# RWKV-7 chunk products on whole 128x128 stationaries, with the group norm's tokens on partitions

## The chip, the cores and the metric

One core of a Trainium2 chip runs the whole program in one launch. The metric is device time in microseconds (us). Five engines take part: TensorE (PE, matmuls, with its weight loads listed as PEld), VectorE (DVE), ScalarE (ACT), GpSimd (POOL) and SyncE (SP), on whose queue all DMAs are issued.

## The reference

One step of a one-layer decoder trunk for 256 prompt tokens and 8 sample sequences of 8 tokens, 320 token columns in all. Three branches (HGRN2, RWKV-7, a short gated convolution) are computed from one input projection, merged by gates, projected, and followed by an MLP. The change is in the RWKV-7 branch, with 16 heads of 64 channels:

```python
def step(S, inp):                      # per token; S is (B, H, 64, 64), [value, key]
    r_, w_, k_, v_, kk_, a_ = inp
    sa = einsum('bhij,bhj->bhi', S, -kk_)
    S = S * w_[:, :, None, :] + sa[..., None] * (kk_ * a_)[:, :, None, :] + v_[..., None] * k_[:, :, None, :]
    return S, einsum('bhij,bhj->bhi', S, r_)
...
mu = mean(o_rw, -1); var = mean(square(o_rw - mu), -1)         # per token and head
o_rw = ((o_rw - mu) * rsqrt(var + 64e-5)) * rw_ln_w + rw_ln_b
bonus = sum(r_ * k_ * rw_r_k, -1) * v_
y_b = ((o_rw + bonus) * g) @ w_pb
```

## The kernel before

Activations lie feature-major: 128 channels on partitions, 320 token columns (256 of the prompt, 64 of the samples). Weights come by DMA in granules of 8 blocks of 128x128 (`granule`, lines 107 to 116). ScalarE casts each granule to a high part `whi_t` (line 104), VectorE subtracts to get the low part `wlo_t` (line 105), and `dense` (lines 118 to 132) issues three matmuls for each block into `mm_t` (lines 128 to 130). These dense matmuls make up most of TensorE's work. Three buffers hold each of raw, high and low parts.

The RWKV branch runs first, with the projections of the short convolution among it. It handles two heads (128 channels) at a time, eight pairs `j`. For each pair:

- `rwkv_front` projects keys, receptances and values, and forms for five chunks of 64 tokens (four of the prompt, one that holds all samples) the operands: `LYR` (alpha, from the decay and kk, and rho, from the receptance), `BK` and its transposed form `BT`, and `X`, which holds token-major values beside the state or the intermediate u. `vx` becomes the bonus term.
- `rwkv_solve` forms the products inside each chunk (line 441, operands of 64 partitions), masks them into `Nb`, `LYR` and `GB`, and inverts I - N into `Pm`.
- `rwkv_chunks` goes through the four prompt chunks in order. For each chunk: alpha times `X` into `yp` (line 534), rho times `X` as the first half of the output in `op` (line 536), a copy `Y` on ScalarE (line 538), `Pm` times `Y` (line 543), two copies on VectorE that put u into `X` (line 545), the new state (line 548), the second half of the output (line 550), and the state with its decay into `X` of the next chunk (lines 555 and 557). Then come the sample chunk (lines 561 to 585) and the group norm (lines 593 to 610).

In the chunk products each head has its own matmul with a stationary operand of 64 columns. The two heads write the two halves of the partitions of one PSUM bank. The output is feature-major, so the norm's mean and variance are products with the block matrix `bo64` (lines 597 and 602), and all its arithmetic runs over 320 columns, a reciprocal among it (`rsqrt`, line 162).

The source fixes which engine does each operation. The order of the queues is not written out: when the program is built, a planner orders each engine's instructions by their dependencies and its own estimate of costs, and it interleaves the dense matmuls of one pair with the small products of another. `X`, `LYR`, `BT` and `W` have two buffers, so front and solve of later pairs run beside the chunks of an earlier one. The tiles `py_t` and `po_t` have one PSUM bank each.

Of the kernel before, what the change touches and what calls it, by code (L numbers as in the profile page):

```python
# [16 lines left out]
# Columns of every feature-major tile: 256 prompt tokens, then 8 sample  # L17
# sequences of 8 tokens each.
# [8 lines left out]
# Tile indices (128 columns each) inside w_in.  # L27
# [5 lines left out]
# Columns of the packed per-channel parameters.  # L33
# [10 lines left out]
# words between two diagonal 16x16 blocks of a [128, 640] array  # L44
# [5 lines left out]
def _constants():  # L50
    """Identity, block matrices and masks: they depend on shapes alone."""
# [6 lines left out]
    cols["bo64"] = cols["bo1"] / 64.0  # L58
    up, upi = (s % 64 < q), (s % 64 <= q)
    same = (s % 64) // 8 == q // 8  # L60
    cols["mkp"] = np.concatenate([up, upi, up], 1)
    cols["mks"] = np.concatenate([up & same, upi & same, up & same], 1)
# [24 lines left out]
class K:  # L87
# [19 lines left out]
    def granule(self, src, pool=None):  # L107
        """8 weight blocks of 128x128 as float32r high and low parts."""
        raw = self.wraw.tile([128, 1024], F32, name="raw")
        self.nc.sync.dma_start(raw, src)  # L110
        hi = (pool or self.whi).tile([128, 1024], F32R, name="whi_t")
        lo = (pool or self.wlo).tile([128, 1024], F32R, name="wlo_t")
        for q in range(2):
            c = slice(512 * q, 512 * q + 512)
            self.split(hi[:, c], lo[:, c], raw[:, c])
        return hi, lo

    def dense(self, granules, ah, al):
        """PSUM tile = sum over the granules of weight block ^T @ activation block."""
# [14 lines left out]
    def dense_wide(self, tiles, ah, al, psp, wpool):  # L134
        """Several column tiles at once, one activation block after the other."""
# [19 lines left out]
    def rsqrt(self, pool, v, tag):  # L155
        """1/sqrt(v): table square root, reciprocal, one Newton step."""
# [12 lines left out]
    # -----------------------------------------------------------------------  # L169
    def build(self):  # L170
# [41 lines left out]
        # operands of the sample sequences' new states wait in DRAM  # L212
# [40 lines left out]
    def shift_mix(self, wp, n, name, packed):  # L253
        """Projected tile n with the token shift mixed in; keeps the last rows."""
# [22 lines left out]
    def rwkv(self, cx):  # L277
# [16 lines left out]
        # tiles whose constant blocks are written once  # L294
# [4 lines left out]
        for nm, cols in (("Nb", 640), ("GB0", 640), ("GB1", 640), ("LX", 256)):  # L299
            Z[nm] = kp.tile([128, cols], F32, name=nm)  # L300
            nc.gpsimd.memset(Z[nm], 0.0)
# [3 lines left out]
        # DRAM scratch through which the diagonal 16x16 blocks change layout  # L305
# [27 lines left out]
    def rwkv_front(self, j, wp, w2):  # L333
# [9 lines left out]
        # decay, gate and rate from the low-rank projections  # L343
# [20 lines left out]
        # normalised kk, k with its rate  # L364
# [8 lines left out]
        LYR = w2.tile([128, 5, 2, 2, 64], F32, name="LYR")  # L373
# [3 lines left out]
        V.tensor_mul(LYR[lo, :, 0, 0, :], ch(Wp)[lo], ch(kkn)[lo])  # L377
        V.tensor_mul(LYR[hi, :, 1, 1, :], ch(Wp)[hi], ch(kkn)[hi])
        G.tensor_mul(LYR[lo, :, 0, 1, :], ch(W)[lo], ch(r)[lo])
        G.tensor_mul(LYR[hi, :, 1, 0, :], ch(W)[hi], ch(r)[hi])  # L380
# [10 lines left out]
        # token-major values: X holds [state or u ; v] per chunk and head  # L391
# [16 lines left out]
        V.tensor_mul(vx, bs[:, :NT], vx)  # L408

        # token-major [beta ; kappa]  # L410
# [10 lines left out]
    def rwkv_solve(self, j, front, wp):  # L421
# [7 lines left out]
        # pairwise products inside each chunk  # L429
        Nb = Z["Nb"].rearrange("p (c w) -> p c w", w=128)  # L430
        GB = Z["GB%d" % (j % 2)].rearrange("p (c h w) -> p c h w", h=2, w=64)
        for mk, cc in (("mkp", slice(0, 4)), ("mks", slice(4, 5))):
# [5 lines left out]
            for i in range(n):  # L438
                c = cc.start + i
                for h, rows in ((0, lo), (1, hi)):  # L440
                    T.matmul(pp[h][:, i, :], BK[rows, c, h:h + 2, :].rearrange("p a w -> p (a w)"),  # L441
                             LYR[rows, c, h].rearrange("p a w -> p (a w)"), start=True, stop=True)
            for h, rows in ((0, lo), (1, hi)):
                p3 = pp[h]
                orow = hi if h == 0 else lo
                ca = lo if h == 0 else hi        # columns of alpha
                cr = hi if h == 0 else lo        # columns of rho
                m = self.cst(mk)[:, 64 * h:64 * h + 128]
                mc = lambda rr, col: m[rr, col].unsqueeze(1).to_broadcast([64, n, col.stop - col.start])
                full = slice(0, 128)  # L450
                V.tensor_mul(Nb[rows, cc, ca], p3[rows, :n, ca], mc(rows, ca))
                V.tensor_mul(LYR[orow, cc, h].rearrange("p c a w -> p c (a w)"), p3[orow, :n, :], mc(orow, full))
# [4 lines left out]
        # P = (I - N)^-1: diagonal 16x16 blocks first, each on one partition  # L457
# [21 lines left out]
        # then doubling, with M = P^T  # L479
# [31 lines left out]
    def rwkv_chunks(self, j, front, wp, w2):  # L511
# [13 lines left out]
        # prompt chunks in order  # L525
        op = self.po.tile([128, 512], F32, name="po_t")
        Y = wp.tile([128, 64], F32, name="Y")
        Sw = wp.tile([128, 64], F32, name="Sw")
        heads = ((0, lo), (1, hi))
        for c in range(4):  # L530
            wc = W[:, c * 64 + 63:c * 64 + 64]
            yp = self.py.tile([128, 512], F32, name="py_t")
            for h, rows in heads:
                T.matmul(yp[rows, 0:64], LYR[:, c, h, h, :], X[:, c, h, :], start=True, stop=True)
            for h, rows in heads:
                T.matmul(op[rows, c * 64:c * 64 + 64], X[:, c, h, :], LYR[:, c, h, 1 - h, :],
                         start=True, stop=False)
            S.copy(Y, yp[:, 0:64])
# [8 lines left out]
            for h, rows in heads:  # L547
                T.matmul(sp[rows, 0:64], BT[:, c, h, :], X[:, c, h, :], start=True, stop=True)
            for h, rows in heads:
                T.matmul(op[rows, c * 64:c * 64 + 64], X[:, c, h, :], GB[:, c, h, :], start=False, stop=True)  # L550
            sn = wp.tile([128, 64], F32, name="sfin")
            for h, rows in heads:
                dst = X[rows, c + 1, h, :] if c < 3 else sn[rows, :]
                if c:
                    V.scalar_tensor_tensor(dst, sp[rows, 0:64], wc[rows], Sw[rows, :], ALU.mult, ALU.add)
                else:
                    V.tensor_scalar_mul(dst, sp[rows, 0:64], wc[rows])
# [3 lines left out]
        LX = Z["LX"].rearrange("p (b h a t) -> p b h a t", h=2, a=2, t=8)  # L561
        for h, rows in heads:
            S.copy(LX[rows, :, h], LYR[rows, 4, h].rearrange("p a (b t) -> p b a t", t=8))
        cp = self.pa.tile([128, 512], F32, name="pa_t")
        for b in range(8):
            T.matmul(cp[lo, b * 32:b * 32 + 32], s0[:, b, :], Z["LX"][:, b * 32:b * 32 + 32],
                     start=True, stop=True)
        cpv = cp[lo, 0:256].rearrange("p (b h a t) -> p b h a t", h=2, a=2, t=8)
        YA = wp.tile([64, 2, 64], F32, name="YA")
        YR = wp.tile([128, 64], F32, name="YR")  # L570
        t8 = lambda t: t.rearrange("p (b t) -> p b t", t=8)
        for h, rows in heads:
            S.copy(t8(YA[:, h, :]), cpv[:, :, h, h, :])
            S.copy(t8(YR[rows, :]), cpv[:, :, h, 1 - h, :])
        yp = self.py.tile([128, 512], F32, name="py_t")
        for h, rows in heads:
            T.matmul(yp[rows, 0:64], LYR[:, 4, h, h, :], X[:, 4, h, :], start=True, stop=False)
            T.matmul(yp[rows, 0:64], YA[:, h, :], ident[lo, lo], start=False, stop=True)
        S.copy(Y, yp[:, 0:64])
        up = self.py.tile([128, 512], F32, name="py_t")  # L580
        T.matmul(up[:, 0:64], Pm[:, 4, :], Y, start=True, stop=True)
        for h, rows in heads:
            V.tensor_copy(X[rows, 4, h, :], up[rows, 0:64])
        for h, rows in heads:
            T.matmul(op[rows, 256:320], X[:, 4, h, :], GB[:, 4, h, :], start=True, stop=True)
# [536 lines left out]
```

## Time and profile before

| | |
|---|---|
| time of 3 runs, median (lowest to highest) | 2500.53 us (2499.78 to 2504.2) |
| profiled execution, span from the first to the last instruction | 2502.3 us |
| mean granted clock of TensorE | 0.992 |
| moved by DMA | 355.02 MB, mean 142 GB/s |

The page gives no other time of the profiled execution than its span; the median of the runs lies 0.07% under it. Rows of the profile give busy time of an engine; for TensorE the listed length of a matmul overlaps with the next one's, so the distance between two starts tells what one costs. Names such as `py_t<-X,LYR 128*64 128x64` give the tile written, the tiles read, rows and columns of the stationary operand, and the shape of the moving one. A float32 product shows as two instructions (x2), a transpose as one. Rows of groups end with busy us, mean ns of one, and idle us before them with what ended the idle time.

### The profile page before, as it was taken

Reading aid. Unit: us, or ns where it says so; the run is one execution under the profiler, and the core shown is the slowest. Engines: PE = TensorE matmul, PEld = TensorE weight load, DVE = VectorE, ACT = ScalarE, POOL = GpSimd, SP = SyncE. Lnnn points to the kernel's source line nnn. Section 1 sums busy time; section 2 is a strip of 40 time slices with the busy share of each in tenths; the row PEclk is TensorE's granted clock in tenths of the full one; section 3 lists DMA queues with packets and bytes.
Section 4 is the critical chain, followed back from the end, with each engine's and each line's share of the span. In section 5 each row is a group of like instructions: output and inputs, shape, how many; then the busy total and the mean of one; then the engine's idle time right before and its main releaser. Section 6 shows DMA issues by size and latency. Waiting matters only on the chain.

```text
span 2502.3 us, 42443 instructions
## 1 busy us (share of the span) xinstructions
PE 2456.1 (98%) x16588; PEld 2337.3 (93%) x16588; DVE 1523.7 (61%) x3022; ACT 980.0 (39%) x1882; POOL 409.4 (16%) x558
## 2 busy tenths in 40 slices
PE   8999999999999999999999999899999999999998
PEld 7887888889999999999999897899999999999997
DVE  6878888786565665565555445854555555555555
ACT  5433434433433333343444334434333333333333
POOL 5423333231000000011111233400000000000003
PEclk9999999999999999999999999899999999999999
DMA  6333333334434344344444655444444444444443
GB/s 215 120 84 89 99 112 122 115 124 127 138 129 137 129 137 131 127 143 148 151 152 147 214 189 184 131 149 151 152 148 150 149 152 152 147 149 151 152 150 129
DMA packets 131703, 355.02 MB, mean 142 GB/s; under 512 B 34864, under 2 KB 43440, under 8 KB 131504
## 3 DMA queue, kind: packets, MB, share of 16 engines
q1 hardware_dynamic: 131504, 352.32, 43.1%
q8 instruction: 131, 2.15, 0.4%
q14 instruction: 68, 0.56, 0.1%
HBM read 337.13 MB, written 15.14 MB: 141 GB/s over the span
## 4 chain that ended last, share of the span: by engine, by line
PE 89%; DVE 7%; POOL 1%; DMA 1%; issue 1%; SPq 0%; ACT 0%; POOLq 0%; DVEq 0%; ACTq 0%
PE mm_t L128 27%; PE mm_t L129 26%; PE mm_t L130 26%; DVE wlo_t L105 1%; PE pi L501 1%; DMA Pm<-dP 1%; PE pi L441 1%; PE pho_t L805 1%; PE plv_t L765 1%; DVE x L941 1%; PE pi L507 1%; PE plv_t L766 0%; DVE hl L943 0%; DVE xl L200 0%; PE po_t L550 0%
## 5 line engine op out<-in xcount | busy, mean ns | idle before, releaser
L104 ACT CAST whi_t<-raw 128x512 fp32r<-128x512 f32 x1192 | 685.1, 619 | 1159.5 <-PE mm_t L129 726.5
L105 DVE TENSOR_TENSOR wlo_t<-raw,whi_t 128x512 fp32r<-128x512 f32 x1192 | 831.5, 727 | 304.2 <-ACT whi_t L104 295.4
L130 PE MATMUL mm_t<-xh,wlo_t 128*128 128x320 f32 x2080 | 656.1, 316 | 1.8 <-DVE wlo_t L105 1.7
L128 PE MATMUL mm_t<-xh,whi_t 128*128 128x320 f32 x2080 | 657.4, 316 | 0.0
L129 PE MATMUL mm_t<-xl,whi_t 128*128 128x320 f32 x2080 | 655.6, 315 | 0.0
L130 PEld LDWEIGHTS mm_t<-xh,wlo_t 128*128 128x128 f32 x2080 | 392.5, 189 | 9.1 <-DVE wlo_t L105 3.0
L128 PEld LDWEIGHTS mm_t<-xh,whi_t 128*128 128x128 f32 x2080 | 392.8, 189 | 8.0 <-issue 0.9
L129 PEld LDWEIGHTS mm_t<-xl,whi_t 128*128 128x128 f32 x2080 | 393.2, 189 | 4.6 <-issue 0.4
L128 PE MATMUL mm_t<-hh,whi_t 128*128 128x320 f32 x1232 | 382.2, 310 | 0.0
L129 PE MATMUL mm_t<-hl,whi_t 128*128 128x320 f32 x1232 | 381.4, 310 | 0.0
L130 PE MATMUL mm_t<-hh,wlo_t 128*128 128x320 f32 x1232 | 381.3, 310 | 0.0
L130 PE MATMUL mm_t<-rh,wlo_t 128*128 128x320 f32 x1024 | 316.8, 309 | 0.0
L128 PE MATMUL mm_t<-rh,whi_t 128*128 128x320 f32 x1024 | 316.8, 309 | 0.0
L129 PE MATMUL mm_t<-rl,whi_t 128*128 128x320 f32 x1024 | 316.8, 309 | 0.0
L128 PEld LDWEIGHTS mm_t<-hh,whi_t 128*128 128x128 f32 x1232 | 231.9, 188 | 6.5 <-ACT sqt L955 4.9
L129 PEld LDWEIGHTS mm_t<-hl,whi_t 128*128 128x128 f32 x1232 | 231.9, 188 | 0.0
L130 PEld LDWEIGHTS mm_t<-hh,wlo_t 128*128 128x128 f32 x1232 | 231.9, 188 | 0.0
L130 PEld LDWEIGHTS mm_t<-rh,wlo_t 128*128 128x128 f32 x1024 | 192.3, 188 | 0.0
L128 PEld LDWEIGHTS mm_t<-rh,whi_t 128*128 128x128 f32 x1024 | 192.3, 188 | 0.0
L129 PEld LDWEIGHTS mm_t<-rl,whi_t 128*128 128x128 f32 x1024 | 192.3, 188 | 0.0
L1024 DVE TENSOR_TENSOR m<-m,mm_t 128x320 f32<-128x320 f32 x112 | 54.7, 488 | 189.4 <-PE mm_t L130 189.4
L956 POOL TENSOR_TENSOR ssf<-ssf,sqt 128x320 f32<-128x320 f32 x14 | 13.9, 993 | 841.7 <-issue 809.6
(410 smaller groups left out, 2762.0 us busy)
## 6 DMA issues: line engine op xcount, KB each, us to landing
raw<-w_in SPq DMA_DIRECT2D x260, 512.0 KB
raw<-w_ff SPq DMA_DIRECT2D x256, 512.0 KB
raw<-w_o SPq DMA_DIRECT2D x32, 512.0 KB
hs<-s_hg SPq DMA_DIRECT2D x16, 512.0 KB
raw<-w_pc SPq DMA_DIRECT2D x16, 512.0 KB
raw<-w_pb SPq DMA_DIRECT2D x16, 512.0 KB
raw<-w_pa SPq DMA_DIRECT2D x16, 512.0 KB
o_hgs<-hsn SPq DMA_DIRECT2D x16, 256.0 KB
```

What stands on the lines that cost most here:

```text
L104: self.nc.scalar.copy(hi, src)
L105: self.nc.vector.tensor_sub(lo, src, hi)
L128: mmul(ps[:, :NT], hi[:, w], ah[:, i, :], start=(i == 0), stop=False)
L129: mmul(ps[:, :NT], hi[:, w], al[:, i, :], start=False, stop=False)
L130: mmul(ps[:, :NT], lo[:, w], ah[:, i, :], start=False, stop=(i == n - 1))
L441: T.matmul(pp[h][:, i, :], BK[rows, c, h:h + 2, :].rearrange("p a w -> p (a w)"), LYR[rows, c, h].rearrange("p a w -> p (a w)"), start=Tru ...
L501: T.matmul(ps[:, half(i)], Nb[:, i, :], cols(Mm[:, i, :], h, 0), start=True, stop=True)
L507: T.matmul(ps[:, half(i)], T3[:, i, :], cols(Pm[:, i, :], h, 1), start=True, stop=True)
L765: T.matmul(ps[:, 0:64], KS[:, 0:128], rh[:, 0:hb], start=True, stop=True)
L805: T.matmul(op[:, 256:320], s0[:, b, :], QX[:, 64 * b:64 * b + 64], start=(b == 0), stop=False)
L941: nc.vector.scalar_tensor_tensor(x1, t, self.par("g2", k), x1, ALU.mult, ALU.add)
L1024: nc.vector.tensor_add(d, d, ps)
```

## The change

Two heads go through the array side by side, on a stationary of 128 columns:

- `LYR` is laid out as [alpha of head 0, alpha of head 1, rho of head 0, rho of head 1], so that `LYR[:, c, 0:2]` and `LYR[:, c, 2:4]` are 128x128 stationaries. The moving operand is `X` of both heads, 128 columns. The result is 128x128, of which the two diagonal 64x64 blocks are used; the others are computed and left.
- The output of a chunk comes out token-major (`ot4`), with rho and `GB` as the stationaries. ScalarE copies the diagonal blocks into `otm`.
- The copy of `Y` becomes two copies, one for each head.
- The sample states are taken two sequences at a time (128x128 stationary, 4 products instead of 8). The selected parts go into a zeroed tile `Ms` by two VectorE copies, and products with the matrix `bi` (two identities side by side) add them to `yp` and to the output `os`.
- The group norm works on `otm`, tokens on partitions: sums by VectorE reductions over 64 channels, statistics of five numbers on each partition. The normed output goes into a zeroed tile `Od`, and five transposes bring it back to channels on partitions, where weight and bonus are applied from PSUM.
- The shift `lnb` is added to the bonus in `rwkv_front`, on ScalarE.
- `bo64` is dropped from the constants, `bi` takes its place, and the masks lose 64 columns each.

Comments were taken out elsewhere; nothing else differs. The core of the diff:

```diff
+        S.activation(vx, vx, AF.Identity, bias=self.par("lnb", j))          # in rwkv_front
...
         for c in range(4):
             wc = W[:, c * 64 + 63:c * 64 + 64]
             yp = self.py.tile([128, 512], F32, name="py_t")
+            T.matmul(yp[:, 0:128], alpha(c), flat(X[:, c]), start=True, stop=True)
+            T.matmul(ot4[:, c, :], rho(c), flat(X[:, c]), start=True, stop=False)
             for h, rows in heads:
-                T.matmul(yp[rows, 0:64], LYR[:, c, h, h, :], X[:, c, h, :], start=True, stop=True)
-            for h, rows in heads:
-                T.matmul(op[rows, c * 64:c * 64 + 64], X[:, c, h, :], LYR[:, c, h, 1 - h, :],
-                         start=True, stop=False)
-            S.copy(Y, yp[:, 0:64])
+                S.copy(Y[rows, :], yp[rows, hb(h)])
...
-            for h, rows in heads:
-                T.matmul(sp[rows, 0:64], BT[:, c, h, :], X[:, c, h, :], start=True, stop=True)
-            for h, rows in heads:
-                T.matmul(op[rows, c * 64:c * 64 + 64], X[:, c, h, :], GB[:, c, h, :], start=False, stop=True)
+            T.matmul(sp[:, 0:128], flat(BT[:, c]), flat(X[:, c]), start=True, stop=True)
+            T.matmul(ot4[:, c, :], flat(GB[:, c]), flat(X[:, c]), start=False, stop=True)
...
+            S.copy(otm[rows, 0:4, :], ot4[rows, :, hb(h)])                  # per head, after the 4 chunks
...
-        for b in range(8):
-            T.matmul(cp[lo, b * 32:b * 32 + 32], s0[:, b, :], Z["LX"][:, b * 32:b * 32 + 32],
-                     start=True, stop=True)
+        for b in range(4):
+            T.matmul(cp[:, b * 64:b * 64 + 64], flat(s0[:, 2 * b:2 * b + 2, :]),
+                     Z["LX"][:, b * 64:b * 64 + 64], start=True, stop=True)
+        for i, rows in heads:
+            V.tensor_copy(Ms[rows, :, :, i, :].rearrange("p q b t -> p b q t"), cpv[rows, :, i, :, :])
...
-        for h, rows in heads:
-            T.matmul(yp[rows, 0:64], LYR[:, 4, h, h, :], X[:, 4, h, :], start=True, stop=False)
-            T.matmul(yp[rows, 0:64], YA[:, h, :], ident[lo, lo], start=False, stop=True)
-        S.copy(Y, yp[:, 0:64])
+        T.matmul(yp[:, 0:128], alpha(4), flat(X[:, 4]), start=True, stop=False)
+        T.matmul(yp[:, 0:128], Z["Ms"][:, 0:128], both, start=False, stop=True)
...
-            T.matmul(op[rows, 256:320], X[:, 4, h, :], GB[:, 4, h, :], start=True, stop=True)
+        T.matmul(os[:, 0:128], Z["Ms"][:, 128:256], both, start=True, stop=False)
+        T.matmul(os[:, 0:128], flat(GB[:, 4]), flat(X[:, 4]), start=False, stop=True)
+            S.copy(otm[rows, 4, :], os[rows, hb(h)])
...
-        T.matmul(mean[:, :NT], self.cst("bo64"), o, start=True, stop=True)
-        V.tensor_sub(o, o, mean[:, :NT])
-        S.activation(sq2, o, AF.Square)
-        T.matmul(var[:, :NT], self.cst("bo64"), sq2, start=True, stop=True)
-        V.tensor_scalar_add(sq2, var[:, :NT], GN_EPS)
-        rstd = self.rsqrt(wp, sq2, "gn")
-        V.tensor_mul(o, o, rstd)
-        V.tensor_scalar(o, o, self.par("lnw", j), self.par("lnb", j), ALU.mult, ALU.add)
-        G.tensor_add(o, o, vx)
+        V.tensor_reduce(sm, otm, axis=AX, op=ALU.add)
+        V.tensor_scalar_mul(sm, sm, 1.0 / 64)
+        V.tensor_sub(otm, otm, wide(sm))
+        S.activation(sq2, otm, AF.Square)
+        V.tensor_reduce(vs, sq2, axis=AX, op=ALU.add)
+        V.tensor_scalar(vs, vs, 1.0 / 64, GN_EPS, ALU.mult, ALU.add)
+        S.activation(ts, vs, AF.Sqrt)
+        V.reciprocal(rt, ts)
+        ...                                  # one Newton step: four operations on [128, 5]
+        for h, rows in heads:
+            V.tensor_mul(Od[rows, :, hb(h)], otm[rows], wide(rt)[rows])
+        for cc in (slice(0, 4), slice(4, 5)):
+            for i in range(n):
+                T.transpose(t3[:, i, :], Od[:, cc.start + i, :], ident)
+            for h, rows in heads:
+                V.scalar_tensor_tensor(o[rows, cc], t3[rows, 0:n, hb(h)], self.par("lnw", j)[rows], vx3[rows, cc],
+                                       ALU.mult, ALU.add)
```

More of the change, by code (lines that the diff above doesn't have):

```diff
@@ L523, in rwkv_chunks @@
         nc.sync.dma_start(lg, io["lg"][:, j * 128:j * 128 + 128])
-        op = self.po.tile([128, 512], F32, name="po_t")
+        heads = ((0, lo), (1, hi))
+        hb = lambda h: slice(64 * h, 64 * h + 64)
+        flat = lambda t: t.rearrange("p h w -> p (h w)")
+        alpha = lambda c: flat(LYR[:, c, 0:2, :])
+        rho = lambda c: flat(LYR[:, c, 2:4, :])
+        ot = self.po.tile([128, 512], F32, name="po_t")
+        ot4 = ot.rearrange("p (c w) -> p c w", w=128)
         Y = wp.tile([128, 64], F32, name="Y")
         Sw = wp.tile([128, 64], F32, name="Sw")
-        heads = ((0, lo), (1, hi))
+        otm = wp.tile([128, 5, 64], F32, name="otm")
         for c in range(4):
@@ L590, in rwkv_chunks @@
                           W[:, 256:320].rearrange("p (b w) -> p b w", w=8)[:, :, 7])
-        o = wp.tile([128, NT], F32, name="o")
-        S.copy(o[:, :NP], op[:, :NP])
-        V.tensor_add(o[:, NP:], op[:, NP:NT], YR)
-        mean = self.pa.tile([128, 512], F32, name="pa_t")
-        T.matmul(mean[:, :NT], self.cst("bo64"), o, start=True, stop=True)
-        V.tensor_sub(o, o, mean[:, :NT])
-        sq2 = wp.tile([128, NT], F32, name="sq2")
-        S.activation(sq2, o, AF.Square)
-        var = self.pa.tile([128, 512], F32, name="pa_t")
@@ new lines, in rwkv_chunks @@
+        V.reciprocal(rt, ts)
+        V.tensor_mul(ts, rt, rt)
+        V.tensor_mul(ts, ts, vs)
+        V.tensor_scalar(ts, ts, -0.5, 1.5, ALU.mult, ALU.add)
+        V.tensor_mul(rt, rt, ts)
+        Od = Z["Od"].rearrange("p (c w) -> p c w", w=128)
+        for h, rows in heads:
+            V.tensor_mul(Od[rows, :, hb(h)], otm[rows], wide(rt)[rows])
+        o = wp.tile([128, 5, 64], F32, name="o")
+        vx3 = vx.rearrange("p (c w) -> p c w", w=64)
+        for cc in (slice(0, 4), slice(4, 5)):
+            n = cc.stop - cc.start
+            tp = self.pa.tile([128, 512], F32, name="pa_t")
+            t3 = tp.rearrange("p (c w) -> p c w", w=128)
+            for i in range(n):
+                T.transpose(t3[:, i, :], Od[:, cc.start + i, :], ident)
+            for h, rows in heads:
+                V.scalar_tensor_tensor(o[rows, cc], t3[rows, 0:n, hb(h)], self.par("lnw", j)[rows], vx3[rows, cc],
+                                       ALU.mult, ALU.add)
```

63 lines of the change are left out of this document (35 added, 28 removed).

## The prediction

> **What bounds the kernel now.** I read the page first, then the work by stage, then who waits for whom, then single stretches of TensorE's timeline. On the page:
>
> ```profile
> PE 2456.1 (98%) x16588; PEld 2337.3 (93%) x16588; DVE 1523.7 (61%) x3022; ACT 980.0 (39%) x1882; POOL 409.4 (16%) x558
> PE 89%; DVE 7%; POOL 1%; DMA 1%; issue 1%; SPq 0%; ACT 0%; POOLq 0%; DVEq 0%; ACTq 0%
> ```
>
> TensorE (PE) is busy for 98% and holds 89% of the chain that ended last. The change lies in the RWKV stage, which fills the first 600 us; its middle 400 us by windows (columns: PE, PEld, DVE, ACT, POOL busy us, then granted clock, DMA share, GB/s):
>
> ```profile
> 150.00:250.00 100.00, 93.78 (x631) 78.88 (x630) 81.02 (x201) 41.78 (x84) 36.22 (x63) 0.97 0.32 83
> 350.00:450.00 100.00, 98.66 (x733) 87.98 (x732) 85.41 (x196) 45.76 (x94) 35.69 (x65) 1.00 0.35 110
> sum 400.00, PE 388.16 PEld 335.44 DVE 329.21 ACT 161.81 POOL 132.28; mean PE 97.04 PEld 83.86 DVE 82.30 ACT 40.45 POOL 33.07
> ```
>
> PE is full here too (97%), because dense projections are issued between the small products. VectorE (DVE) is second with 82%. Is it late for the weights that it splits? The waits of the same 400 us say no:
>
> ```profile
> ACT whi_t L104 <- PE mm_t L129: 80.7, 39, 4.5
> ```
>
> ScalarE, which starts each split, stands 80.7 us waiting for PE to give a weight buffer back. The split weights lie ready ahead of PE, so PE time taken out of this stage should shorten the kernel. The question is what the touched products cost PE, and that is not their listed duration, since matmuls are pipelined. I take starts. One chunk step (columns: start, length, then the group):
>
> ```profile
> 267.55 0.31 PE L128 MATMUL mm_t<-xh,whi_t 128*128 128x320 f32 x1
> 267.79 0.33 PE L536 MATMUL po_t<-LYR,X 128*64 128x64 f32 x2
> 268.05 0.42 PE L129 MATMUL mm_t<-xl,whi_t 128*128 128x320 f32 x1
> 268.39 0.34 PE L534 MATMUL py_t<-X,LYR 128*64 128x64 f32 x4
> 268.56 0.28 PE L536 MATMUL po_t<-LYR,X 128*64 128x64 f32 x2
> 268.77 0.41 PE L130 MATMUL mm_t<-xh,wlo_t 128*128 128x320 f32 x1
> 269.02 0.31 PE L128 MATMUL mm_t<-xh,whi_t 128*128 128x320 f32 x1
> 269.18 0.35 PE L543 MATMUL py_t<-Y,Pm 128*128 128x64 f32 x2
> 269.34 0.39 PE L129 MATMUL mm_t<-xl,whi_t 128*128 128x320 f32 x1
> 269.57 0.31 PE L130 MATMUL mm_t<-xh,wlo_t 128*128 128x320 f32 x1
> ...
> 271.70 0.33 PE L536 MATMUL po_t<-LYR,X 128*64 128x64 f32 x2
> ```
>
> A float32 product is two instructions, so the two heads of L534 are x4. A dense matmul undisturbed starts 0.147 us after the one before. From 267.55 to 269.02 stand three dense ones, 0.44 us; the other 1.03 us are the L534 and L536 products of one chunk. The product L543 on a whole 128x128 stationary costs 269.02 to 269.57 less 0.29, which is 0.26 us, though it waits for a copy just the same. A stationary of 64 columns costs extra whenever PE comes to it from a 128-wide one and goes back: L536's two instructions alone take 267.55 to 268.05 less 0.15, 0.35 us.
>
> **The change part by part.** The new products have a 128x128 stationary and 128 moving columns in float32. The trace has this shape in the HGRN stage, again between dense matmuls:
>
> ```profile
> 641.24 0.31 PE L130 MATMUL mm_t<-bh,wlo_t 128*128 128x320 f32 x1
> 641.38 0.38 PE L781 MATMUL plv_t<-QP,KS 128*128 128x128 f32 x2
> 641.52 0.39 PE L128 MATMUL mm_t<-bh,whi_t 128*128 128x320 f32 x1
> 641.75 0.31 PE L129 MATMUL mm_t<-bl,whi_t 128*128 128x320 f32 x1
> ```
>
> 641.24 to 641.75 less two dense ones (0.29) is 0.22 us for such a product. That is the price I use.
>
> *Chunk steps, 32 of them (8 pairs of heads, 4 chunks).* Alpha and rho: two products of 0.22, 0.44 us, for the 1.03 above. Walking the timeline from 50 to 600 us, 21 chunks stand so, in two groups; 3 in one group (0.58), and 8 in one run with 64-row products, where no switch of their own is paid (0.35). Saved: 21 x 0.59 + 3 x 0.14 - 8 x 0.09 = 12.1 us. State and second output (L548, L550): 22 in two groups at the same 1.03, 8 in one at 0.59, 2 in longer runs: 22 x 0.59 + 8 x 0.15 - 2 x 0.09 = 14.0 us. L543 stays.
>
> *Sample sequences.* The four products L577 and L578:
>
> ```profile
> 275.69 0.31 PE L128 MATMUL mm_t<-xh,whi_t 128*128 128x320 f32 x1
> 275.93 0.33 PE L577 MATMUL py_t<-X,LYR 128*64 128x64 f32 x2
> ...
> 276.95 0.41 PE L129 MATMUL mm_t<-xl,whi_t 128*128 128x320 f32 x1
> 277.21 0.31 PE L130 MATMUL mm_t<-xh,wlo_t 128*128 128x320 f32 x1
> ```
>
> 275.69 to 277.21 less 0.29 is 1.23 us; two full products take 0.44: 0.79 x 8 = 6.3 us. L585 stands as two lone groups of the L536 kind (2 x 0.35, and 0.11 that the dense matmul after it is late): 0.81 to 0.92 for a pair, against 0.44 for the two products into `os`: 0.42 x 8 = 3.4 us. The state products L566:
>
> ```profile
> 313.33 1.12 PE L566 MATMUL pa_t<-LX,s 128*64 128x32 f32 x16
> ```
>
> 16 starts in some 0.9 us (0.06 each) become 8 of 0.11, which is 0.88: nothing where they share a run with other small tiles (six pairs), 0.8 us in the two where they stand alone: 1.6 us.
>
> *Group norm.* Two products with the block matrix go, five transposes come.
>
> ```profile
> 342.74 0.31 PE L129 MATMUL mm_t<-xl,whi_t 128*128 128x320 f32 x1
> 342.88 0.70 PE L597 MATMUL pa_t<-o,c 128*128 128x320 f32 x2
> 343.18 0.55 PE L130 MATMUL mm_t<-xh,wlo_t 128*128 128x320 f32 x1
> 343.57 0.31 PE L128 MATMUL mm_t<-xh,whi_t 128*128 128x320 f32 x1
> 249.25 0.60 PE L497 MATMUL pi<-c,Pm 128*128 128x128 f32 x4
> ```
>
> 342.74 to 343.57 less 0.29 is 0.54 us, and L602 is the same product: 1.08. Transposes are one instruction each; four of L497 start within about 0.33 us (0.60 less the last one's 0.27), 0.11 each, so five cost 0.55. Saved 0.53 x 8 = 4.2 us.
>
> PE together: 12.1 + 14.0 + 6.3 + 3.4 + 1.6 + 4.2 = 41.6 us.
>
> *VectorE.* Per pair the reciprocal and seven other 320-wide or 64-wide operations go; the statistics shrink to five numbers a row.
>
> ```profile
> L162 DVE RECIPROCAL gn_y<-gn_t 128x320 f32<-128x320 f32 x8 | 17.1, 2142 | 0.0
> L605 DVE TENSOR_TENSOR o<-o,gn_y 128x320 f32<-128x320 f32 x7 | 3.9, 561 | 0.0
> L595 DVE TENSOR_TENSOR o<-po_t,YR 128x64 f32<-128x64 f32 x8 | 1.8, 225 | 4.8 <-ACT o L594 4.8
> L555 DVE SCALAR_TENSOR_TENSOR X<-py_t,W,Sw 64x64 f32<-64x64 f32 x30 | 8.5, 283 | 5.2 <-PE py_t L548 4.5
> L973 DVE TENSOR_TENSOR rm_t<-rm_y x1: 149/149/149, 1548.0 to 1548.0; 128x3 f32<-128x3 f32 x1
> ```
>
> Gone: 2.14, six at about 0.5 and L595 at about 0.25: 5.4 us. New: seven tiny ones at 0.16 (L973), 1.1; the subtraction and the two half-height scalings at about 0.5, 1.5; two copies and four fused operations out of PSUM at 0.3 to 0.4 (L555 and up), 2.0; two reductions, which the trace does not have: they read 320 columns, so between 0.3 and, at worst, half the reciprocal, 1.1; I take 0.5, by L605, the nearest. Sum 5.6, between 5.2 and 6.8: even, +0.2 us per pair. DVE is not on PE's path while the buffers are ahead, but the same DVE work now falls into a shorter stage, and I put 2 us in all on it.
>
> *ScalarE* gains small work: per chunk the copy of Y becomes two, one per head, five in a pair. One is
>
> ```profile
> L538 ACT COPY Y<-py_t 128x64 f32<-128x64 f32 x30 | 6.3, 212 | 48.7 <-PE py_t L534 48.6
> ```
>
> 0.21 us. It lies on the chain of a chunk (Y before L543); behind it in ACT's queue stand casts of weights. The queue has 60% idle, and the row shows it waiting 48.6 us for PE at this very place; the cover is the dense work that PE does meanwhile. Without it: 40 x 0.21 = 8 us. The shift by `lnb` moves into `rwkv_front` as one 320-wide ScalarE operation, before the chunks need `vx`. GpSimd loses three operations a pair and gains two memsets at the start, in front of which nothing of the chunks waits. On PE the five transposes wait for the whole norm, as L597 and L602 did for its parts, and dense matmuls stand behind them; `self.B`, which ends the norm, is read only after the stage. No DMA is added; on SP's queue only the constants shrink by 128 columns.
>
> So -41.6 + 2 = -40 us. The profiled execution spans 2502.3 us, 0.07% above the median of the runs, 2500.5: 2462 there, 2460 against the median.
>
> **The rivals.**
>
> *A: VectorE sets the pace.* It has 82% of these 400 us and none of its work goes. With 41.6/8 = 5.2 us less for each of about six pairs in there, 400 becomes 369, and DVE 330 of 369, 89%. For it: the order on DVE is fixed when the program is built, so a chain step can stand in front of a split. Against: 85.41 of 100 us in the fullest stretch left PE at 98.66, and the 80.7 us of waiting on PE is over twice the 31 us to be taken out. If DVE could not rise above its 82%, only the two pairs outside would gain, 10 us: 2490. Halfway: 2475.
>
> *B: slower, the switch is not what is paid.* If the 0.24 us before each narrow group were the wait for its operand and not the narrow shape, it would stay, and only the streaming would count: a two-head product on narrow tiles takes two starts of 0.06, 0.12 us, a full one 0.22. Per chunk four such products: +0.42 us, x 32 = +13.4; L585 +2.6; L566 and the norm -4.6: 2500.5 + 11 = 2512. It decides as soon as more than three quarters of the extra remain. Against: L543 and L597 wait for operands too and cost no more than their columns. The Trainium skill, TensorEngine Tiling (Array Packing), Overview, speaks for it: sides of 64 or less run up to twice as fast as separate tiles, so giving tiles up would cost. The same page, Key Properties, says that a change of tiling mode drains the array; by that the gain holds, and the 0.35 us of a lone L536 group agrees.
>
> *C: the change does nothing.* PE's freed time turns to waiting, since each chunk's chain (alpha, copy, L543, copy, state) has to run 32 times in order: 2500. Against: chunk steps follow each other in 3.9 us where nothing hinders them (L536 at 267.79 and 271.70), so four take 16 of a pair's 65 us; the chain has room.
>
> *D: the clock.* The windows show 0.97 in 150 to 250: PE ran below full clock for a few us. If idle spells of PE bring that on, fewer of them give back up to 5 us over the stage, and new ones take as much; it moves the result inside the range, and has no chance of its own.
>
> **How the numbers follow.** The PE sum in force, 2446 to 2475: 0.68. Its lower end takes all of the clock's 5 us, the upper mark of L585 and half a dozen us of the switches in mixed runs; its upper end leaves out the Y copies' cover and half of A. A in full, 2475 to 2495: 0.18. Below 2446: 0.03. C: 0.05. B, or an order of the queues that loses more than it gains: 0.06. The range of 2446 to 2490 leaves out 0.03 below and about 0.15 above. What a measurement here can tell from no change is about 0.2%, 5 us: faster 0.89, same 0.05, slower 0.06.
>
> **What would show it.** A chunk's alpha and rho as two x2 groups 128*128 with 128 columns, costing 0.44 us over the dense ones around them. The RWKV stage ends near 560 and not 600; everything after it keeps its length. PE busy stays near 97% in the stage and DVE's share goes to about 89%; casts wait less for PE, some 50 us. The prediction is wrong if the starts around the new groups still show the 0.24 us hole, if waits of PE for wlo_t or for Y come up by tens of us, or if the reductions take over 1 us.

## The result, and the profile after

The changed kernel takes 2475.97 us (median of 4 runs, 2475.11 to 2477.07), the kernel before in the same session 2501.81 us (4 runs, 2499.78 to 2504.2): a ratio of 0.9895, 95% interval 0.9881 to 0.9909. That is 26 us faster where 40 us were forecast. The profiled execution spans 2473.3 us (before 2502.3), its mean granted clock is 0.995. Of all executions below, one of the kernel before without its chain took 3901 us at a granted clock of 0.55, and it is left out of that kernel's time.

The page of the changed kernel, the middle 400 us of the RWKV stage by windows (columns as before), and ScalarE's wait for a weight buffer in the same 400 us:

```profile
PE 2425.8 (98%) x16244; PEld 2326.5 (94%) x16244; DVE 1513.2 (61%) x3102; ACT 989.9 (40%) x1919; POOL 384.4 (16%) x536
PE 89%; DVE 8%; POOL 1%; issue 1%; ACT 1%; DMA 0%; SPq 0%; ACTq 0%; DVEq 0%; POOLq 0%
150.00:250.00 100.00, 95.95 (x641) 83.57 (x641) 86.86 (x242) 46.48 (x101) 29.92 (x59) 1.00 0.30 95
350.00:450.00 100.00, 97.23 (x673) 88.69 (x672) 83.87 (x227) 42.87 (x96) 30.82 (x61) 1.00 0.36 116
sum 400.00, PE 385.32 PEld 346.48 DVE 331.05 ACT 175.39 POOL 119.16; mean PE 96.33 PEld 86.62 DVE 82.76 ACT 43.85 POOL 29.79
ACT whi_t L104 <- PE mm_t L129: 94.6, 41, 5.9
```

Read against before: TensorE (PE) fell from 97.04 to 96.33 busy us per 100, VectorE (DVE) went from 82.3% to 82.8%, and the casts wait 94.6 us for PE where they waited 80.7. PE is still what the weights wait for; yet it is a little less full.

Where does the saved time lie? The first operation behind the RWKV stage is a transpose of the HGRN stage (its line moved from L736 to L767). TensorE's timeline of the changed kernel, then of the kernel before:

```profile
600.51 0.27 PE L767 MATMUL ptr_t<-c,hv 128*128 128x128 f32 x1
```

```profile
626.87 0.27 PE L736 MATMUL ptr_t<-c,hv 128*128 128x128 f32 x1
```

26.4 us were saved up to here. (The prediction put the end of the stage near 600 us; the convolution that goes with the last pair runs on to 627.) The HGRN stage keeps its length; the other 2.6 us of the two spans lie after it, where PE ran less at a lower clock. So nearly the whole question is inside the RWKV stage. One chunk step of the changed kernel on PE (start, length, group; L543 alpha, L544 rho, L551 Pm times Y, L555 state, L556 second output):

```profile
256.47 0.31 PE L129 MATMUL mm_t<-xl,whi_t 128*128 128x320 f32 x1
256.61 0.31 PE L130 MATMUL mm_t<-xh,wlo_t 128*128 128x320 f32 x1
257.01 0.46 PE L543 MATMUL py_t<-X,LYR 128*128 128x128 f32 x2
257.30 0.39 PE L544 MATMUL po_t<-X,LYR 128*128 128x128 f32 x2
257.45 0.39 PE L128 MATMUL mm_t<-xh,whi_t 128*128 128x320 f32 x1
257.68 0.31 PE L129 MATMUL mm_t<-xl,whi_t 128*128 128x320 f32 x1
258.05 0.44 PE L551 MATMUL py_t<-Y,Pm 128*128 128x64 f32 x2
258.29 0.39 PE L130 MATMUL mm_t<-xh,wlo_t 128*128 128x320 f32 x1
258.52 0.30 PE L128 MATMUL mm_t<-xh,whi_t 128*128 128x320 f32 x1
...
259.10 0.31 PE L129 MATMUL mm_t<-xl,whi_t 128*128 128x320 f32 x1
259.32 0.46 PE L555 MATMUL py_t<-X,BT 128*128 128x128 f32 x2
259.61 0.39 PE L556 MATMUL po_t<-X,GB 128*128 128x128 f32 x2
259.76 0.39 PE L130 MATMUL mm_t<-xh,wlo_t 128*128 128x320 f32 x1
259.99 0.31 PE L128 MATMUL mm_t<-xh,whi_t 128*128 128x320 f32 x1
```

The forecast looked for alpha and rho at 0.44 us over the dense matmuls. Here it is 256.61 to 257.68 less two dense starts of 0.147, 0.78 us: the dense matmul at 256.61 is followed after 0.40 us instead of 0.147. Pm costs 257.68 to 258.52 less 0.29, 0.55 us, and state with output 0.60. I counted every such place of both kernels (from the last dense start before the group to a dense start behind it, less 0.147 for each dense matmul). Before, the groups cost the same nearly everywhere: 0.68 and 0.35 for the two groups of a half step, half of the places within 0.005 us of that. Now the least is the forecast price to the hundredth for alpha with rho and for state with output (0.443 each; Pm, which did not change, has 0.218), but the costs scatter from there to over 0.8 us; the means are 0.627, 0.469 and 0.637. Waits are part of it. The queue of weight loads (PEld), which a product passes first, shows for 50 to 600 us what it stood idle for at the norm's transposes (L635), at Pm (L551) and at Pm of the samples (L589), with us in total, times, longest:

```profile
PEld pa_t L635 <- DVE Od L625: 7.9, 8, 1.8
PEld py_t L551 <- ACT Y L546: 6.7, 21, 0.6
PEld py_t L589 <- ACT Y L587: 3.3, 8, 0.5
```

In the kernel before, the same view lists no wait for Y at all. (The 11 us for Y and the 13.7 us for Od in the expectations below add idle time of PE and of PEld, which overlap.)

Added up per class over the eight pairs (mean cost times count, us; up to six of 32 chunk steps stand in one group with products of front or solve, and are taken like the others):

| | forecast | measured |
|---|---|---|
| alpha and rho, 32 chunks | -12.1 | -11.2 (0.98 to 0.63 each) |
| state and second output, 32 | -14.0 | -9.0 (0.92 to 0.64) |
| Pm, 32 | 0 | +7.3 (0.24 to 0.47) |
| samples: `yp`, `os`, states | -11.3 | -8.3 |
| Pm of the samples, 8 | 0 | +3.3 (0.22 to 0.64) |
| norm: two products, then five transposes | -4.2 | +3.3 (1.08 to 1.49) |
| sum | -41.6 | -14.6 |

The stage gained 26.4, so 12 us came from elsewhere. Counted without classes, from the first dense matmul to the transpose above (each distance between two dense starts, less 0.147): groups of chain and norm products alone gave 13.1 us, groups of front and solve alone 14.4, dense matmuls among themselves 4.1, and groups that hold both kinds cost 5.7 more. Part of this is the clock: PE stood at half the clock for 6.8 us of the stage instead of 17.1, worth up to 5.1.

### The profile page after: what moved, and what is told of

Read it like the earlier page. It is cut to its first block, busy times and chain, and to the rows that moved or that the text cites. A ratio compares the mean times of both kernels' runs of the same rounds, so it can differ in the third digit from the quotient of the medians.

```text
span 2473.3 us, 41923 instructions
## 1 busy us (share of the span) xinstructions
PE 2425.8 (98%) x16244; PEld 2326.5 (94%) x16244; DVE 1513.2 (61%) x3102; ACT 989.9 (40%) x1919; POOL 384.4 (16%) x536
## 4 chain that ended last, share of the span: by engine, by line
PE 89%; DVE 8%; POOL 1%; issue 1%; ACT 1%; DMA 0%; SPq 0%; ACTq 0%; DVEq 0%; POOLq 0%
PE mm_t L128 26%; PE mm_t L130 26%; PE mm_t L129 26%; DVE wlo_t L105 1%; PE pi L443 1%; PE pi L503 1%; PE pho_t L836 1%; PE plv_t L796 1%; DVE x L972 1%; PE plv_t L797 1%; PE pi L509 0%; DVE hl L974 0%; DVE xl L200 0%; DVE Pd L476 0%; PE py_t L551 0%
```

## The experiments

Theory 1: the new products cost what was forecast, but PE now reaches the next link of a chain before its operand is there and waits: the narrow groups' holes are gone, in which ScalarE and VectorE had worked, and Y takes two copies. Theory 2: VectorE sets the pace. Where an expectation names a third, it gives its number there. All ratios are to runs of the kernel before on the same chip.

**Narrow alpha and state again** (rho, output, samples and norm as changed; one copy of Y for both heads):

```diff
-  T.matmul(yp[:, 0:128], alpha(c), flat(X[:, c]), ...)
+  T.matmul(yp[rows, 0:64], LYR[:, c, h, :], X[:, c, h, :], ...)      # per head
-  S.copy(Y[rows, :], yp[rows, hb(h)])                                # per head
+  S.copy(Y, yp[:, 0:64])
-  T.matmul(sp[:, 0:128], flat(BT[:, c]), flat(X[:, c]), ...)
+  T.matmul(sp[rows, 0:64], BT[:, c, h, :], X[:, c, h, :], ...)       # per head
```

> The changed kernel with two of its products put back on narrow stationaries, one per head: alpha (into yp) and the state (into sp); Y is one copy again. All else stays. Theory 1 (the prices of the sum hold, and 16 us of the 42 came back as waits of TensorE for operands that come from the chain): each narrow group costs a switch again, 0.35 us or more where a full product is 0.22, 64 times, which is +10 to +25 us, less what the holes cover of the waits for Y and X (up to 10): 2480 to 2495. Theory 2 (VectorE's share sets the pace): VectorE's work is the same, so 2473 to 2479. Theory 3 (narrow groups cost nothing extra, the gain came from the norm and the samples): 2465 to 2476, since two streams of 0.06 are shorter than one product of 0.22.

Measured 2468.65 us (2467.18 to 2470.77), 0.9866, interval 0.9851 to 0.9881: not slower but 7 us faster than the changed kernel, a miss for theory 1's number and inside that of the third. PE's timeline:

```profile
203.61 0.31 PE L129 MATMUL mm_t<-xl,whi_t 128*128 128x320 f32 x1
203.85 0.34 PE L556 MATMUL py_t<-X,BT 128*64 128x64 f32 x4
204.11 0.49 PE L557 MATMUL po_t<-X,GB 128*128 128x128 f32 x2
204.36 0.39 PE L130 MATMUL mm_t<-xh,wlo_t 128*128 128x320 f32 x1
204.59 0.31 PE L128 MATMUL mm_t<-xh,whi_t 128*128 128x320 f32 x1
```

State and output cost 203.61 to 204.59 less 0.29, 0.69 us, and half of the places lie within 0.006 us: the hole is back with the narrow shape. But Pm fell to 0.32 and alpha with rho stayed at 0.62, so a chunk step costs 1.66 us here and 1.73 in the changed kernel, though at its least prices it would cost some 1.5 here and 1.10 there. PEld's view lists no wait for Y at Pm here.

**One full copy of Y** (128 columns, Pm on 128 columns; the unused blocks are carried along):

```diff
-  S.copy(Y[rows, :], yp[rows, hb(h)])            # per head
+  S.copy(Y, yp[:, 0:128])
-  T.matmul(up[:, 0:64], Pm[:, c, :], Y, ...)
+  T.matmul(up[:, 0:128], Pm[:, c, :], Y, ...)
```

> The changed kernel with one copy of Y again, of all 128 columns: Pm is block-diagonal, so Pm times the full Y holds the wanted blocks on its diagonal, and VectorE takes them from there. Same results. Theory 1 (TensorE waits for Y, 11 us in the rows of L551 and L589, because the second copy lengthens the chain and the dense matmuls between are few): the waits for Y at least halve, and the time falls by 3 to 8 us, to 2468 to 2473. Theory 2 (VectorE's share): no VectorE work changes, 2474 to 2478.

Measured 2475.1 us (2474.8 to 2477.22), 0.9893 (0.9877 to 0.991): no change, a miss for theory 1's 3 to 8 us. The copy took 0.27 us instead of 0.44 for two, but the planner then put one dense matmul instead of two between alpha and Pm, and Pm cost 0.55 us.

**The norm's tail later** (transposes, weight, bonus and gate written behind the short convolution, in a function of their own):

```diff
-  self.rwkv_chunks(j, st[j], wp, w2)
+  od = self.rwkv_chunks(j, st[j], wp, w2)
   for i in SC_ORDER[j]: self.short_conv(i)
+  self.rwkv_tail(j, st[j], od, wp)
```

> The changed kernel with the end of a pair's norm (five transposes, weight and bonus, gate) written behind the pair's short convolution, so that dense matmuls of the convolution can go ahead of the transposes. Same work. Theory 1 (TensorE waits for Od, 13.7 us in the rows of L635): these waits go for pairs 1 to 7, and the time falls by 4 to 9 us, to 2467 to 2472. Theory 2: 2474 to 2478.

Measured 2474.91 us (2473.04 to 2476.4), 0.989 (0.9875 to 0.9905): the runs overlap with those of the changed kernel, and theory 1's 4 to 9 us did not come. The wait for Od fell only from 7.9 to 6.0 us.

**Seven of fifteen substitution steps** on VectorE:

```diff
-  for u in range(15, 0, -1):
+  for u in range(7, 0, -1):
```

> The changed kernel with 7 of 15 steps of the substitution on the 16x16 blocks, so the last rows of each block's inverse are left incomplete. Each step is two VectorE operations of some 0.2 us on 40 partitions: VectorE loses 16 a pair, 3.4 us, 27 us in all, and TensorE's work is the same. Theory 1: VectorE is not the pace; the solve's chain gets shorter, which no TensorE row waits for by more than 4 us: 2470 to 2477. Theory 2 (VectorE's share sets the pace): most of the 16 us that are missing come back, 2458 to 2466.

Measured 2470.91 us (2469.85 to 2475.07), 0.9877 (0.9863 to 0.9892). VectorE's share of the middle 400 us:

```profile
sum 400.00, PE 385.51 PEld 348.07 DVE 318.24 ACT 175.65 POOL 121.11; mean PE 385.51 PEld 348.07 DVE 318.24 ACT 175.65 POOL 121.11
```

PE is as busy as in the changed kernel with 12.8 us less on VectorE, and 5 us are gained for 26 taken out of the whole stage. Theory 2 falls as the main cause. What the 5 us are, the shorter solve or VectorE's queue, this run can't tell.

**Dense matmuls fixed between the steps.** `fill(n)` issues n blocks (three matmuls each) of the pair's own short convolution behind the last chain product, and the next chain product behind them; pair 0 has no convolution.

```diff
+  with self.fill(2):                                     # first kernel: before Pm only
       T.matmul(up[:, 0:64], Pm[:, c, :], Y, ...)
+  with self.fill(2 if c else 0):                         # second and third: before alpha too,
       T.matmul(yp[:, 0:128], alpha(c), ...)
+  with self.fill(3):                                     # and before the state and the last output
       T.matmul(sp[:, 0:128], flat(BT[:, c]), ...)
+  hook()    # third: the norm's tail of pair j, behind the key projection of pair j + 2
```

> The changed kernel, with six dense matmuls of the same pair's short convolution (0.88 us of PE work that has to be done anyway) fixed between the alpha and rho products and the Pm product of every chunk and of the sample step, in pairs 1 to 7 (pair 0 has no short convolution). Theory 1 (PE now arrives at the chain's products before their operands; a Pm group costs 0.47 us instead of its 0.22, since only one or two dense matmuls stand in front of it): in 35 steps the 0.25 us go, 9 us at most, less where the next link of the chain waits instead: 2468 to 2473 us, Pm groups near 0.25. Rival, VectorE or the splits set the pace and the order on PE does not matter: 2474 to 2479.

> As the kernel with the fill before Pm, and in addition six dense matmuls fixed before the alpha products of chunks 1 to 3 and nine before the state products and before the last output of the samples. Theory 1: the waits before alpha and rho (0.627 less 0.44) and before state and output (0.636 less 0.44) go as well, 0.19 + 0.20 us in 28 chunks, 11 us, on top of the 9 of Pm, part of it lost in pair 0 and at places where the convolution's blocks run out: 2458 to 2467 us. Rival, the order on PE does not matter: 2474 to 2479; or the fixed order keeps PE behind casts of split weights: above 2480.

> As the kernel with all fills, and the norm's five transposes (1.49 us a pair against a price of 0.55, PE waiting for Od) stand behind a dense projection of 48 matmuls of the pair after next. Theory 1: 0.9 us in seven pairs, 5 to 6 us, go too: 2452 to 2462 us. Rival, the order on PE does not matter: 2474 to 2479.

Measured 2570.94 us (ratio 1.0278, 1.0264 to 1.0292), 2602.16 us (1.0397, 1.0383 to 1.0412) and 2588.23 us (1.0341, 1.0325 to 1.0357): 95 to 126 us slower, against every expectation. The windows 120 to 160 us of the first one (fill before Pm), then of the changed kernel:

```profile
120.00:140.00 20.00, 13.55 (x62) 11.58 (x60) 4.15 (x10) 2.31 (x4) 1.92 (x3) 0.57 0.25 87
140.00:160.00 20.00, 12.76 (x42) 9.65 (x42) 8.86 (x33) 1.98 (x8) 2.64 (x6) 0.50 0.06 18
```

```profile
120.00:140.00 20.00, 20.00 (x145) 18.75 (x144) 10.97 (x27) 4.59 (x9) 1.52 (x2) 1.00 0.35 124
140.00:160.00 20.00, 19.69 (x132) 17.32 (x131) 16.67 (x56) 8.03 (x23) 8.86 (x17) 1.00 0.30 99
```

And PE in it (L531 the first transposes of pair 1's solve; then the bare chain of pair 0: L588, L589 state and output, L575, L576 alpha and rho, L584 Pm):

```profile
124.01 1.12 PE L531 MATMUL pi<-c,Pm 128*128 128x128 f32 x4 [3.50 <-DMA Pm<-dP]
...
144.98 0.77 PE L588 MATMUL py_t<-X,BT 128*128 128x128 f32 x2 [1.57 <-DVE X L586]
145.54 0.63 PE L589 MATMUL po_t<-X,GB 128*128 128x128 f32 x2
146.53 0.76 PE L575 MATMUL py_t<-X,LYR 128*128 128x128 f32 x2 [0.36 <-DVE X L596]
147.09 0.64 PE L576 MATMUL po_t<-X,LYR 128*128 128x128 f32 x2
147.82 0.69 PE L584 MATMUL py_t<-Y,Pm 128*128 128x64 f32 x2
149.23 0.77 PE L588 MATMUL py_t<-X,BT 128*128 128x128 f32 x2 [0.73 <-DVE X L586]
```

Between 124 and 160 us there is not one dense matmul: the next ones in line, those of pair 1's convolution, were tied to pair 1's chunks, and the solve of pair 1 and the chunks of pair 0, which have dense work around them in the changed kernel, stood bare. The clock fell to half in the 3.50 us of idle time before L531; in the whole stage PE stood at half clock for 147 us (174 and 171 in the other two kernels), 140 more than in the changed kernel, which is worth up to 70 of the 101 us that the stage grew. So dense work is one supply for all chains of the stage, and what is tied to one is missing at another. It says nothing on whether PE's waits at the chunk steps could be filled by work that is not needed elsewhere.

**Alpha alone narrow** (the first two edits of the first experiment, state as changed):

```diff
-  T.matmul(yp[:, 0:128], alpha(c), ...)
+  T.matmul(yp[rows, 0:64], LYR[:, c, h, :], X[:, c, h, :], ...)      # per head; one copy of Y
```

> The changed kernel with alpha alone narrow again (two 64-wide products per chunk, one copy of Y for both heads), state, rho, samples and norm as changed. If what made the run with narrow alpha and narrow state 7 us faster is the hole of a narrow alpha group plus the single copy (both on the Y hop), it shows here too, and the state products at their full price add to it: 2465 to 2469 us. If it came from the narrow state: 2474 to 2478.

Measured 2471.46 us (2471.12 to 2473.91), 0.9877 (0.9864 to 0.9891): between the two. Alpha's side (the hop to Y) gives some 4.5 of the 7 us; the runs, made in different sessions, don't overlap with either neighbour, but the intervals do. A chunk step costs 0.75 + 0.31 + 0.58 = 1.64 us. With one copy of Y and the narrow product the hop is short again: in the first experiment, in this one and in the kernel before 0.65 us pass from the start of alpha to the end of Y, in the changed kernel 1.00 (medians of 32).

**Without the chain**, in the changed kernel and in the kernel before, and with one hop taken out:

```diff
-  T.matmul(yp[:, 0:128], alpha(c), flat(X[:, c]), ...);  S.copy(Y[rows, :], yp[rows, hb(h)])
+  T.matmul(yp[:, 0:128], alpha(c), flat(BT[:, c]), ...); S.copy(Y[rows, :], BT[rows, c, h, :])
-  T.matmul(up[:, 0:64], Pm[:, c, :], Y, ...)
+  T.matmul(up[:, 0:64], Pm[:, c, :], BT[:, c, 0, :], ...)
   # all chain products, copies and transposes alike; the one-hop kernel: only the copies of Y and Pm
```

> The changed kernel without its chain: the same instructions in number, engine and shape, but the chunk and sample products, the Y, u and state copies and the five transposes read tiles of the pair that have long been ready (BT in place of X and Y and of the PSUM results, Pm in place of Od), so nothing waits for a step of the chain; the output leaves the recurrence out. This gives the price of the new products alone. Theory 1 (PE pays about 0.6 us a chunk and most of the norm's 1.49 us for waiting on operands): alpha and rho 0.44, Pm 0.22, state and output 0.44 instead of 0.63, 0.47 and 0.64, so 0.63 x 32 = 20 us, Pm of the samples 0.4 x 8 = 3, norm 0.9 x 8 = 7; 30 at most, 20 at least: 2446 to 2456 us. Rival, the missing 16 us are not waits on the chain (VectorE's pace, or the price of the products among other work): 2468 to 2476.

> The kernel before without its chain, in the same way (BT for X and Y, W for the operands of the norm's two products). It tells how much of its narrow groups' price was the narrow shape and how much the wait for operands. Theory 1 (the hole is paid for the shape; Pm cost 0.24 with no wait): it keeps most of its time, 2480 to 2500 us, and stays 30 us or more above the changed kernel without its chain. Rival, a good part of the hole was the wait for the operand: 2455 to 2470 us, and within 15 us of the changed kernel without its chain.

> The changed kernel with one hop of the chain taken out: the Y copies and the Pm products read BT, so Pm no longer waits for alpha's result; all else stays a chain; the output leaves that step out. Theory 1: Pm groups fall from 0.47 and 0.64 to about 0.22, 8 + 3 us: 2464 to 2468 us; if the wait only moves to the next hop (state behind X): 2470 to 2476 us, with state and output above 0.64. Rival, waits do not matter: 2474 to 2478.

Measured: changed kernel without the chain 2497.71 us (0.998, 0.9971 to 0.9988), kernel before without it 2507.17 us (1.0027, 1.0014 to 1.0039), changed kernel with the Y hop out 2478.57 us (0.9903, 0.9891 to 0.9916). All three expectations of theory 1 missed: taking waits away by force gained nothing. Of the rivals, that of the one-hop kernel (waits do not matter, 2474 to 2478) comes closest; and the two kernels without a chain lie under 10 us apart, where theory 1 asked for 30 or more and the rival for less than 15. With the Y hop out, Pm ran straight behind alpha and rho, the three costing 0.99 us together instead of 1.10, and state with output rose to 0.70; PE's waits for X at the state products went from 2.2 us to 4.1:

```profile
PE py_t L555 <- DVE X L553: 4.1, 6, 0.9
```

Without the whole chain the planner put the four chunks of a pair into one run with single dense matmuls between, and the solve and the next front lost them as cover. Groups of the solve and of the front, from 50 to 600 us (the last figures are the idle time before them): the changed kernel, then the same without its chain:

```profile
L499 PE MATMUL pi<-c,Pm 128*128 128x128 f32 x64 | 9.7, 275 | 0.0
L417 PE MATMUL pa_t<-c,BK 64*128 64x64 f32 x80 | 7.5, 232 | 5.2 <-DVE t L474 3.3 <-DVE BK L387 1.8
```

```profile
L499 PE MATMUL pi<-c,Pm 128*128 128x128 f32 x64 | 9.9, 277 | 9.1 <-DMA Pm<-dP 9.1
L417 PE MATMUL pa_t<-c,BK 64*128 64x64 f32 x80 | 8.5, 254 | 14.6 <-DVE t L474 7.4 <-DVE BK L387 7.1
```

Half clock rose from 6.8 to 30.7 us, and in the kernel before from 17.1 to 44.4. So the totals compare orders of the queues as much as waits, and decide neither theory. One wait was also left in: `py_t` has a single bank, and each product into it waits for the one before. In the changed kernel without its chain, the loads of alpha and Pm show it:

```profile
PEld py_t L543 <- PE py_t L555: 1.3, 7, 0.2
PEld py_t L551 <- PE py_t L543: 0.9, 5, 0.2
```

These runs do settle what a narrow group costs when nothing is waited for. The kernel before without its chain, a narrow group and then a dense matmul in the like place, and what the loads of alpha waited for ("issue" is time in which the profile shows no wait):

```profile
379.03 0.42 PE L130 MATMUL mm_t<-xh,wlo_t 128*128 128x320 f32 x1
379.37 0.34 PE L534 MATMUL py_t<-BT,LYR 128*64 128x64 f32 x4
379.64 0.42 PE L128 MATMUL mm_t<-xh,whi_t 128*128 128x320 f32 x1
...
381.22 0.42 PE L128 MATMUL mm_t<-xh,whi_t 128*128 128x320 f32 x1
381.48 0.31 PE L129 MATMUL mm_t<-xl,whi_t 128*128 128x320 f32 x1
PEld py_t L534 <- issue: 5.5, 26, 0.4
```

From the dense start to the narrow one pass 0.34 us, to a dense matmul in the like place, behind a narrow group too, 0.26. Alpha alone costs (379.03 to 379.64 less 0.147) 0.458 to 0.465 us in 18 places. Rival B of the prediction (the hole is a wait) is excluded by that. The page "TensorEngine Tiling (Array Packing)" of the Trainium skill, section Key Properties, has such a change of mode drain the array; these places agree.

**Narrow alpha and state with the later tail:**

```diff
   # the edits of the first and the third experiment together
```

> The two edits that each gave something put together: alpha and state narrow, and the norm's tail (transposes, weight, bonus, gate) written behind the short convolution. If their gains add (7 and 1 us): 2466 to 2468 us; if the late tail does nothing here: 2468 to 2470.

Measured 2470.2 us (2468.8 to 2472.03), 0.9873 (0.986 to 0.9885): nothing on top of the first. That one, with 2468.65 us, is the fastest of all that ran.

## Why the prediction was right in sign and 16 us off in size

- *The bound.* Right: PE's time in the RWKV stage moved the end; 26.4 of the 29.0 us between the two spans lie there. The forecast was 2460 us and the measured time 2476, inside the range of 2446 to 2490; but it lies just in the band that was set aside for rival A (2475 to 2495), which did not happen, so that the range held is in part luck.
- *The price of the products.* Right as a least price: 0.443 us for two products occurs as forecast, and the hole belongs to the narrow shape. Wrong as a sum: the step "state and second output" gave 9.0 of 14.0 us, with a mean of 0.64 for the 0.44.
- *The steps costed at nothing* failed. The Y copies "cover" was to be the dense work meanwhile, with 8 us if it is gone: Pm cost 7.3 us more, and 3.3 more at the samples. The five transposes were to wait "as L597 and L602 did": they cost 1.49 us a pair for a price of 0.55, so the term of -4.2 became +3.3. Between alpha and Pm lie two dense matmuls, 0.29 us, before and after alike; that was all the cover, and it just sufficed for one copy. Pm starts within 0.06 us of the end of Y in 23 of 32 chunks, in the kernel before in 2. In the prediction's stretch Pm starts 0.79 us after alpha (268.39 to 269.18) with Y ready 0.19 us earlier (median); in the stretch above it starts 1.04 us after (257.01 to 258.05), 0.05 us after Y. The two copies span 0.44 us for 0.21, and the whole product takes longer than the narrow one. The number was at hand (40 x 0.21); the step that failed was to set it aside for a cover that I had read from ScalarE's waiting, not from the slack of Y before Pm.
- *What nobody counted* gave 12 us back: less half clock (up to rival D's full 5 us) and cheaper groups of solve and front. PE's largest waits there in the kernel before, 7.1 us for `xsv` at L396 and 3.5 us for the DMA of Pm at L497, are 0.3 us and none in the changed one. That this helped is luck: nothing in the prediction led to it, and why the new order is kinder to these products is not shown.
- *Rival C* (freed time turns to waiting, 0.05) came true in part. The prediction held against it that four steps of 3.9 us take 16 of a pair's 65 us; but that room lies outside the steps, and within them PE has only the dense matmuls that the queue holds there, as the count of steps below shows.
- *VectorE* (rival A). The time is what "halfway" of A gave (2475), but its share did not rise (82.8%, not 89%), and 26 us less of its work gave only 5. The two reductions took 0.48 us each for a forecast of 0.5:

```profile
L606 DVE TENSOR_REDUCE gs<-otm 128x5 f32<-128x320 f32 x8 | 3.9, 484 | 0.5 <-ACT otm L596 0.4
L613 DVE TENSOR_REDUCE gv<-sq 128x5 f32<-128x320 f32 x8 | 3.8, 474 | 0.6 <-ACT sq L611 0.6
```

- *The signs named beforehand.* The stage shortened by 26 us and not 40; casts wait longer for PE, not less; waits for Y came up, by 10 us and not by tens; a gap before alpha does remain at many places (0.40 us in the stretch above).

What the experiments show: six kernels whose chain is whole or lacks one hop (the changed one, full Y, fewer substitution steps, narrow alpha, narrow alpha and state, the Y hop out) all pay 1.64 to 1.79 us per chunk step, while the least prices run from 1.10 to some 1.5. In the changed kernel what is taken off the price turns into waiting, and its trace shows why: there the chain itself often runs without slack. Alpha starts within 0.17 us of the last copy into X in 19 of 24 steps, and Pm follows Y at once, as said. 12 of the 24 steps, from alpha to alpha, last 3.4 to 3.9 us, and all but one of these hold 11 to 15 dense matmuls, 1.6 to 2.2 us; the rest goes to the chunk step, whatever its products cost. With alpha and state narrow, Pm meets Y that closely in one chunk of 32, the short steps last 3.1 to 3.8 us, and some 1.5 of the 1.66 us are price: that all six are alike is in part chance.

What stays open is whether an order with more dense matmuls in each step would gain: no run had one without taking them from the solve. Why narrow state products save another 3 us, where they cost 0.11 us more a step, was not found either.

## What to carry to other kernels

What an edit adds to a hop between two products of a chain is covered only by the slack that the later product has in the trace; read that slack at the place itself, and cost what exceeds it in full. When independent work covers several chains, tying it to one uncovers another, so look at the neighbour's waits and the granted clock, not only at the step that was helped. A price read at undisturbed places is a lower bound for a step on a chain. And places that all cost the same are not thereby free of waits: a wait for a product of fixed length is the same everywhere, so look at what the weight load was released by.

## What the runs showed of the hardware

- A lone narrow group of two float32 products between single dense matmuls costs 0.44 us (state, 25 places) to 0.46 us (alpha, 18 places) in the kernel before without its chain. Alpha waits for nothing there; the load of the state products at 380.35 us starts 0.12 us after the end of what it waited for, and not 0.04 as where a wait decides.
- One whole product in the same surroundings, in the changed kernel without its chain, costs 0.35 (state, 9 places) and 0.40 us (alpha, 4) instead of the 0.22 read in a long dense run, and these places agree within 0.002 us; yet it is a wait. The load of alpha at 368.19 us starts 0.04 us after the end of the product before it in `py_t`, 0.14 us after the end of the load before it.
- A group of two products on whole stationaries costs 0.44 us at the least, with one of them narrow (two heads) 0.68 (the first experiment): 0.24 us for the whole stationary.
- In the first kernel with fixed dense matmuls the clock fell to half in an idle time of 3.5 us (3.8 between PE starts) and stayed there for 41 us, though in the window 140 to 160 us PE was busy for 12.76 of 20 us and no two starts lay over 2.0 us apart. The Trainium skill, "TensorE: Matmul & The Clock Gate", HAM oscillation, names idle gaps of over about 3.4 us as what lowers the clock. This fall agrees; but in the kernel before the clock also fell at idle times of 2.3 and 2.5 us (they end at 237.9 and 295.5 us, the falls are at 237.7 and 295.8), and here it did not return while the gaps were shorter. So in this case shorter gaps lowered it too, and short gaps went with keeping it low.
